# Where the seventh block product of a pair goes in the plain pair behind it

## The chip, the cores and the metric

The kernel runs on one core of a Trainium2 chip. The metric is the time of one execution in device microseconds: the median of three runs was 879.56 us (879.17 to 882.7). One further execution was taken with the hardware profiler.

## The reference, cut to what matters

The kernel computes one layer of a hybrid block on an input of 512 tokens by 1024 channels, in float32. The part that matters here is the feed-forward half at its end:

```
h   = rmsnorm(x, ffn_pre_norm)
up  = causal_dwconv(h @ w_ffn_up, ffn_conv_w, ffn_conv_b)     # (512, 6144), 3 taps
f_gate, f_val = split(up, 2)                                  # 3072 channels each
f   = (gelu(f_gate) * f_val) @ w_ffn_down
x   = x + rmsnorm(f, ffn_post_norm)
```

The rest of the layer (a Mamba-2 mixer, a gated linear recurrence, their gated merge and an output product) runs before it and is not touched.

## The kernel before, in words

**Arithmetic.** Every matrix product is made of three TensorE products. A weight is split into a high part (`whi`, a cast by ScalarE) and the rest (`wlo`, a subtraction by VectorE), the activations likewise, and high by high, high by low and low by high are added in PSUM.

**The up stage.** The up product goes by 24 pairs (`n` = 0 to 23): 128 gate channels and the 128 value channels that belong to them, over 512 tokens. Pairs 0 and 1 go by whole slabs. The others go by blocks: the pair's weights are a 2 by 2 matrix of blocks (a11, a12 for the gate, a21, a22 for the value), the activations are halves of channels and of tokens. There are two ways.

- A *pair of seven* (`seven`, line 1009 on) uses seven block products in place of eight, with sums of blocks as weights (s1, s2, s3, s4) and sums of activations (`comb`). Six stand in its own six slots, in the order a11, s2, s4, s3, a12, s1; each is 12 matmuls of 256 columns. The seventh, a22 times `comb[3]`, is left over: `last_product` adds it into the right half of the pair's bank `z` while the next pair runs.
- A *plain pair* (`eight`, line 1050 on) has four jobs of 12 matmuls of 512 columns: two fill the bank `oa` (gate) and two fill `ob` (value).

Pairs 2 and 3 are plain, and from pair 4 on the pattern is seven, seven, plain: pairs 6, 9, 12, 15, 18 and 21 are plain, and each of them follows a pair of seven. Pair 22 and 23 are pairs of seven.

**What is done for the pair before.** While pair `n` runs, the pair before it (`old`) is finished in four parts: `gate_part` (convolution of the gate: one ScalarE activation, two VectorE taps), `gelu_part`, `last_product` (the TensorE product named above, for a pair of seven alone) and `value_part`. For a pair of seven `value_part` first adds the seventh product to a sum (line 1005, VectorE), then convolves (ScalarE activation, two taps with the weights `negw`), and then multiplies gate and value (line 866). At the end of its own slots a pair of seven makes its two outputs with VectorE: `oa` gets its right half at line 1045, `ob` at line 1046. Line 1046 reads the right half of `z`, into which `last_product` will add.

**Weights.** `w_split` (line 958 on) runs five blocks ahead of the product that uses the block. For a pair of seven VectorE adds s2 = s1 + a11 (line 965) and s4 = s2 + a12 (line 968), ScalarE casts, VectorE subtracts (line 952). The pair's own 1 MB of weights is loaded into one of two halves of a ring named `H` (line 926), issued by SyncE once the half has been read for the last time; s1 and s3 are each loaded as one block and a second block added by a DMA from GpSimd (lines 940 and 942).

**What sets the order.** TensorE and ScalarE run in the order in which the code is written. VectorE's order in this stage is made by a scheduler from the same code, and so can differ from it: it takes line 965 of the second pair ahead early, as the rows show. Each engine works through its own list in order: an instruction that waits holds up all behind it on that engine. In PSUM, line 1031 reads the right half of the bank `x`, whose left half the product with a12 writes next.

Of the kernel before, what the change touches and what calls it, by code (L numbers as in the profile page):

```python
# [56 lines left out]
def block_kernel(ctx: ExitStack, tc, x, slabs, wgate, pc, rows, out):  # L57
# [12 lines left out]
    def ps():  # L70
        return psum.tile([P, S], F32, tag="ps", name="ps")
# [16 lines left out]
    def mm3(acc, lhi, llo, rhi, rlo, start, stop):  # L88
        mm(acc, lhi, rhi, start, False)
        mm(acc, lhi, rlo, False, False)  # L90
        mm(acc, llo, rhi, False, stop)
# [770 lines left out]
    def f_gate(gt):  # L862
        A.activation(gt, gt, AF.Gelu_apprx_tanh)
# [34 lines left out]
    def block_product(out, w, b, start=False):  # L898

        for k in range(HK):  # L900
            c = slice(k * P, (k + 1) * P)
            for e, (u, v) in enumerate(((0, 0), (0, 1), (1, 0))):
                PE.matmul(out, lhsT=w[u][:, c], rhs=b[v][:, k, :], start=start and k == e == 0,
                          stop=k == HK - 1 and e == 2, skip_group_check=not start)
# [86 lines left out]
    def gate_part(n):  # L991
        p = pr[n]
        p["g"] = conv(p["oa"], pcs[:, C_FCW + 3 * n:C_FCW + 3 * n + 3], C_FCB + n, 3)

    def gelu_part(n):
        f_gate(pr[n]["g"])

    def last_product(n):
        if seven_of[n]:
            block_product(pr[n]["z"][:, T1], blk[n]["wa22"], comb[3])  # L1000

    def value_part(n):
        p = pr.pop(n)
        if seven_of[n]:
            V.tensor_add(p["ob"][:, T0], p["u2"], p["z"][:, T1])
            w = negw[:, 3 * n:3 * n + 3]
        else:
            w = pcs[:, C_FCW + 3 * (NF + n):C_FCW + 3 * (NF + n) + 3]
        vt = conv(p["ob"], w, C_FCB + NF + n, 3)
        f_done(n, p["g"], vt)  # L1010
# [38 lines left out]
    def eight(n, old):  # L1049
        p = pr.setdefault(n, {})  # L1050
        for e, o in enumerate(("oa", "ob")):
            p[o] = acc = ps()
            for h in range(2):
                w = blk[n]["wa%d%d" % (e + 1, h + 1)]
                for k in range(HK):
                    c = slice(k * P, (k + 1) * P)
                    mm3(acc, w[0][:, c], w[1][:, c], h2T[0][:, HK * h + k, :],
                        h2T[1][:, HK * h + k, :], h == k == 0, h == 1 and k == HK - 1)
                if old:
                    if e == h == 0:  # L1060
                        gate_part(old)
                    elif e == 0:
                        gelu_part(old)
                        last_product(old)
                    elif h == 0:
                        value_part(old)
                yield

# [42 lines left out]
    for n in range(PLAIN, NF):  # L1111
        for slot, _ in enumerate((seven if seven_of[n] else eight)(n, old)):
            w_split(g + RING - 1)
            g += 1
            if slot == 0:
                pair_load(n + 2)
                pair_sums(n + 2)
            if n == PLAIN and slot in (1, 2):
                h_split(3 * (slot - 1))
            if n < NF - 1:  # L1120
                continue
            if slot == 2:
                stream.update(load=DOWN_SLAB + 2, split=DOWN_SLAB + 2, use=DOWN_SLAB)
                end[0] = slabs.shape[0]
                load_slab()
            elif slot == 3:
                f_split(0)
                f_split(1)
            elif slot == 5:
                f_split(2)  # L1130
                f_split(3)
        old = n
# [100 lines left out]
```

## Time and profile before

| | us |
|---|---|
| median of three runs | 879.56 |
| lowest, highest | 879.17, 882.7 |
| the profiled execution, whole | 882.06 |
| its span from first to last instruction | 880.4 |
| TensorE busy in the span | 864.7 |
| VectorE busy | 587.4 |
| ScalarE busy | 433.6 |

The mean granted TensorE clock was 0.996 of full speed. The profiled execution is 2.5 us above the median; 1.7 us of its time lie around the span. A view of waits names who waited, for whose instruction, and three numbers: microseconds in total, times, longest. A timeline row begins with start and duration in microseconds; in square brackets stands how long the engine was idle before, and what ended that. "PE" is TensorE's matmul, "PEld" its loading of weights, DVE is VectorE, ACT ScalarE. A matmul's row lasts longer than the step to the next row, since matmuls are pipelined: 512 columns follow each other every 0.23 us and 256 columns every 0.12 us.

### The profile page before, as it was taken

To read this page: it belongs to the slowest core of one execution; us is meant where nothing else is said; L and a number is where in the kernel's file an instruction comes from. 1 tells how busy PE (TensorE), PEld (TensorE's weight loads), DVE (VectorE), ACT (ScalarE), POOL (GpSimd) and SP (SyncE) were. 2 spreads that over 40 slices of the span, in tenths; PEclk is the share of its full clock that TensorE was granted. 3 is DMA by queue.
4 is the path that set the end of the run, shared out by engine and by line. 5 is a ranking of instruction groups with operands and counts; after the bars stand their busy time and mean duration, and the time that the engine had idled before them with its cause. 6 is when DMAs were issued, how large, how long until landed. Compare 5 with 4: busy or idle time off the path is not lost.

```text
span 880.4 us, 11591 instructions
## 1 busy us (share of the span) xinstructions
PE 864.7 (98%) x4554; PEld 739.7 (84%) x4554; DVE 587.4 (67%) x909; ACT 433.6 (49%) x714; POOL 28.4 (3%) x44
## 2 busy tenths in 40 slices
PE   7999999999999999999999999999999999999996
PEld 6888887888878888888888989889999899888885
DVE  6777657987875553444466797878978898743225
ACT  6444545578574443322365565445545556633222
POOL 0000000000000000000000101011011000000000
PEclk9999999999999999999999999999999999999999
DMA  6242223222334422222251837466556543422212
GB/s 225 96 146 96 96 94 110 90 84 79 119 103 174 154 96 96 87 99 101 97 191 25 212 127 195 126 180 170 165 144 181 156 127 113 144 96 95 96 48 96
DMA packets 36007, 108.47 MB, mean 123 GB/s; under 512 B 3632, under 2 KB 6896, under 8 KB 35440
## 3 DMA queue, kind: packets, MB, share of 16 engines
q1 hardware_dynamic: 30864, 99.34, 32.7%
q0 software_dynamic: 5088, 8.39, 5.7%
q8 instruction: 35, 0.57, 0.2%
q14 instruction: 20, 0.16, 0.1%
HBM read 103.49 MB, written 2.13 MB: 120 GB/s over the span
## 4 chain that ended last, share of the span: by engine, by line
PE 75%; DVE 11%; DMA 7%; ACT 5%; issue 2%; SPq 0%; DVEq 0%; ACTq 0%
PE ps L53 75%; DMA H<-slabs 5%; DVE wlo L952 2%; DVE tmp L226 2%; ACT whi L53 1%; DVE wlo L183 1%; ACT L L53 1%; DVE L L644 1%; DMA raw<-slabs 1%; ACT tmp L53 1%; DVE tmp L662 1%; DVE raw L965 0%; DMA wg<-wgate 0%; DVE L L638 0%; ACT junk L247 0%
## 5 line engine op out<-in xcount | busy, mean ns | idle before, releaser
L53 PE MATMUL ps<-H,whi 128*128 128x512 f32 x720 | 224.8, 395 | 0.4 <-DVE H L53 0.4
L183 DVE TENSOR_TENSOR wlo<-raw,whi 128x1024 fp32r<-128x1024 f32 x93 | 113.6, 1223 | 117.3 <-ACT whi L53 115.0
L53 ACT CAST whi<-raw 128x1024 fp32r<-128x1024 f32 (+1 forms) x144 | 127.5, 891 | 100.2 <-PE ps L53 96.6
L53 PE MATMUL ps<-C,whi 128*128 128x256 f32 (+1 forms) x656 | 166.5, 335 | 0.1
L53 PEld LDWEIGHTS ps<-H,whi 128*128 128x128 f32 x720 | 134.3, 188 | 30.3 <-issue 2.4
L53 PE MATMUL ps<-H,wlo 128*128 128x512 f32 x352 | 137.5, 391 | 0.4 <-DVE wlo L183 0.4
L53 PEld LDWEIGHTS ps<-C,whi 128*128 128x128 f32 x656 | 112.0, 190 | 12.6 <-DVE quad L1031 0.3
L53 PE MATMUL ps<-C,wlo 128*128 128x512 f32 (+1 forms) x360 | 122.2, 339 | 0.0
L53 PE MATMUL ps<-L,whi 128*128 128x256 f32 (+1 forms) x400 | 87.2, 300 | 0.0
L53 PE MATMUL ps<-whi,H 128*128 128x512 f32 x256 | 81.5, 394 | 0.0
L226 DVE SCALAR_TENSOR_TENSOR tmp<-ps,pcs,tmp 128x511 f32<-128x511 f32 (+2 forms) x100 | 74.5, 745 | 8.1 <-ACT tmp L53 7.2
L53 PEld LDWEIGHTS ps<-H,wlo 128*128 128x128 f32 x352 | 66.2, 188 | 15.3 <-DVE wlo L183 1.2
L53 PEld LDWEIGHTS ps<-C,wlo 128*128 128x128 f32 x360 | 68.3, 190 | 7.6
L53 PEld LDWEIGHTS ps<-L,whi 128*128 128x128 f32 x400 | 64.4, 191 | 2.5
L53 PEld LDWEIGHTS ps<-whi,H 128*128 128x128 f32 x256 | 48.1, 188 | 10.4 <-issue 0.5
L53 ACT ACTIVATE tmp<-tmp 128x512 f32<-128x512 f32 x36 | 22.7, 632 | 55.3 <-DVE tmp L226 55.3
L53 PE MATMUL ps<-wlo,H 128*128 128x512 f32 x128 | 49.8, 389 | 0.0
L952 DVE TENSOR_TENSOR wlo<-H,whi 128x512 fp32r<-128x512 f32 (+1 forms) x46 | 41.1, 894 | 9.7 <-ACT whi L53 9.6
L53 PE MATMUL ps<-L,wlo 128*128 128x256 f32 x168 | 47.5, 283 | 0.0
L53 ACT ACTIVATE tmp<-ps,halfb 128x512 f32<-128x512 f32 x32 | 21.5, 687 | 49.6 <-PE ps L53 49.6
L53 ACT ACTIVATE tmp<-ps,pcs 128x512 f32<-128x512 f32 x40 | 31.0, 776 | 27.9 <-PE ps L53 27.9
L53 PE MATMUL ps<-Y,whi 128*128 128x512 f32 x128 | 40.5, 397 | 0.2 <-DVE Y L200 0.2
(207 smaller groups left out, 1315.3 us busy)
## 6 DMA issues: line engine op xcount, KB each, us to landing
raw<-slabs SPq DMA_DIRECT2D x103, 512.0 KB, 3.2
H<-slabs SPq DMA_DIRECT2D x23, 1024.0 KB, 5.4
raw<-slabs SPq DMA_DIRECT2D x23, 256.0 KB, 3.8
raw<-slabs POOLq DMA_DIRECT2D x23, 256.0 KB, 6.5
quad<-x SPq DMA_DIRECT2D x8, 512.0 KB, 4.2
M<-acsD SPq DMA_DIRECT2D x4, 1024.0 KB, 4.6
out<-tmp SPq DMA_DIRECT2D x8, 256.0 KB, 2.0
third<-slabs SPq DMA_DIRECT2D x5, 256.0 KB, 6.3
```

Source lines behind the costliest of these rows:

```text
L53: return lambda *args, **kw: self.tc.keep_in_program_order(op(*args, **kw))
L183: V.tensor_sub(*late.pop(0))
L226: V.scalar_tensor_tensor(out=t[:, d:], in0=acc[:, :S - d], scalar=w[:, taps - 1 - d:taps - d], in1=t[:, d:], op0=ALU.mult, op1=ALU.add)
L644: V.tensor_tensor_scan(out=qq[:, e, :], data0=aa[:, e, :], data1=uu[:, e, :], initial=0.0, op0=ALU.mult, op1=ALU.add)
L662: V.tensor_mul(gl, gl, hs[i // 4][:, i % 4, :])
L952: V.tensor_sub(lo, src, hi.bitcast(F32))
```

## The change

In `eight`, the parts for the pair before are handed out differently. Before, `gelu_part` and `last_product` both came behind the second job, and `value_part` behind the third. Now the second job is followed by `gelu_part` alone, the third by `last_product`, the fourth by `value_part`. Nothing is added or removed.

```
                     elif e == 0:
                         gelu_part(old)
+                    elif h == 0:
                         last_product(old)
-                    elif h == 0:
+                    else:
                         value_part(old)
```

In plain pair 3, whose `old` is plain, only `value_part` moves. In pairs 6, 9, 12, 15, 18 and 21 `last_product` moves too. Two places in the order show it. Pair numbers do not stand in the rows; the places are those of pair 6.

On TensorE, before, around the leftover product of pair 5 (`ps_4367` is its bank `z`, `a22_4239` its weights); `ps_4485` is `oa` and `ps_4537` is `ob` of pair 6:

```order
L53 MATMUL ps_4485<-C_3363,whi_4066 128x512
L53 MATMUL ps_4485<-C_3364,whi_4066 128x512
L53 MATMUL ps_4485<-C_3363,wlo_4067 128x512
L53 MATMUL ps_4367<-L_4159,a22_4239 128x256 x12
L53 MATMUL ps_4537<-C_3363,whi_4070 128x512
L53 MATMUL ps_4537<-C_3364,whi_4070 128x512
L53 MATMUL ps_4537<-C_3363,wlo_4071 128x512
```

and now, where `ps_4525` is `ob` of pair 6:

```order
L53 MATMUL ps_4525<-C_3363,whi_4070 128x512
L53 MATMUL ps_4525<-C_3364,whi_4070 128x512
L53 MATMUL ps_4525<-C_3363,wlo_4071 128x512
L53 MATMUL ps_4367<-L_4159,a22_4234 128x256 x12
L53 MATMUL ps_4525<-C_3363,whi_4070 128x512
L53 MATMUL ps_4525<-C_3364,whi_4070 128x512
L53 MATMUL ps_4525<-C_3363,wlo_4071 128x512
```

The product has moved behind the third job's 12 matmuls; what stands on either side of it is now the same bank.

On VectorE, the same pair, before; the row ahead of these is line 965 of pair 8, the row behind them line 1031 of pair 7. `tmp_4477` is `ob` of pair 5, `tmp_4551` its value; `tmp_4589` is the gate of pair 6; `wlo_4067` takes s4 and s3 of pair 7, `wlo_4071` its a12 and s1:

```order
L1005 TENSOR_TENSOR tmp_4477<-quad_3967,ps_4367 128x256
L952 TENSOR_TENSOR wlo_4067<-raw_4174,whi_4066 128x512
L968 TENSOR_TENSOR raw_4174<-raw_4174,H_3964 128x512
L226 SCALAR_TENSOR_TENSOR tmp_4551<-tmp_4477,negw_3968,tmp_4551 128x511
L952 TENSOR_TENSOR wlo_4067<-raw_4124,whi_4066 128x512
L226 SCALAR_TENSOR_TENSOR tmp_4551<-tmp_4477,negw_3968,tmp_4551 128x510
L952 TENSOR_TENSOR a22_4239<-H_3964,a22_4239 128x512
L866 TENSOR_TENSOR H_3965<-tmp_4498,tmp_4551 128x512
L952 TENSOR_TENSOR wlo_4071<-H_3964,whi_4070 128x512
L226 SCALAR_TENSOR_TENSOR tmp_4589<-ps_4485,pcs_88,tmp_4589 128x511
L952 TENSOR_TENSOR wlo_4071<-raw_4199,whi_4070 128x512
L226 SCALAR_TENSOR_TENSOR tmp_4589<-ps_4485,pcs_88,tmp_4589 128x510
```

and now, between the same two rows (`tmp_4567` is the value of pair 5):

```order
L952 TENSOR_TENSOR wlo_4067<-raw_4174,whi_4066 128x512
L952 TENSOR_TENSOR wlo_4067<-raw_4124,whi_4066 128x512
L968 TENSOR_TENSOR raw_4174<-raw_4174,H_3964 128x512
L1005 TENSOR_TENSOR tmp_4477<-quad_3967,ps_4367 128x256
L952 TENSOR_TENSOR a22_4234<-H_3964,a22_4234 128x512
L226 SCALAR_TENSOR_TENSOR tmp_4567<-tmp_4477,negw_3968,tmp_4567 128x511
L952 TENSOR_TENSOR wlo_4071<-H_3964,whi_4070 128x512
L226 SCALAR_TENSOR_TENSOR tmp_4567<-tmp_4477,negw_3968,tmp_4567 128x510
L226 SCALAR_TENSOR_TENSOR tmp_4589<-ps_4485,pcs_88,tmp_4589 128x511
L866 TENSOR_TENSOR H_3965<-tmp_4498,tmp_4567 128x512
L226 SCALAR_TENSOR_TENSOR tmp_4589<-ps_4485,pcs_88,tmp_4589 128x510
L952 TENSOR_TENSOR wlo_4071<-raw_4199,whi_4070 128x512
```

The same twelve instructions stand there; line 1005 went from the first to the fourth place, and only one instruction is left between it and the first tap that needs ScalarE's answer to it. On ScalarE the activation of `value_part` went behind the casts of s3 and a22.

## Rows read from the trace of the kernel before

**Rows 1.** The page: busy us, share of the span, instructions.

```profile
PE 864.7 (98%) x4554; PEld 739.7 (84%) x4554; DVE 587.4 (67%) x909; ACT 433.6 (49%) x714; POOL 28.4 (3%) x44
```

**Rows 2.** Busy time by stretch: length, PE, PEld, DVE, ACT, POOL, clock, DMA.

```profile
532.00:747.00 215.00, 212.13 (x1479) 198.06 (x1478) 181.33 (x305) 115.71 (x200) 19.62 (x23) 1.00 0.56 156
```

**Rows 3.** Waits of TensorE, up stage: total us, times, longest.

```profile
PE ps L53 <- DVE tmp L1046: 2.8, 3, 1.1
PEld ps L53 <- DVE tmp L1046: 4.4, 4, 1.5
...
PEld ps L53 <- DVE quad L1031: 0.3, 1, 0.3
```

**Rows 4.** Timeline: leftover products in plain pairs 6, 9, 15, 18, 21.

```profile
557.03 1.70 PE L53 MATMUL ps<-L,a 128*128 128x256 f32 x12 [0.85 <-DVE tmp L1046]
...
589.60 1.69 PE L53 MATMUL ps<-L,a 128*128 128x256 f32 x12 [0.89 <-DVE tmp L1046]
...
652.10 1.70 PE L53 MATMUL ps<-L,a 128*128 128x256 f32 x12
...
684.53 1.70 PE L53 MATMUL ps<-L,a 128*128 128x256 f32 x12 [1.06 <-DVE tmp L1046]
...
715.71 1.60 PE L53 MATMUL ps<-L,a 128*128 128x256 f32 x12
```

**Rows 5.** Timeline of VectorE from plain pair 6 into pair 7.

```profile
553.51 1.22 DVE L952 TENSOR_TENSOR wlo<-H,whi 128x1024 fp32r<-128x1024 f32 x1
...
556.57 0.41 DVE L1046 TENSOR_TENSOR tmp<-ps,quad 128x256 f32<-128x256 f32 x1
...
561.64 0.69 DVE L965 TENSOR_TENSOR raw<-third,H 128x512 f32<-128x512 f32 x1 [2.03 <-DMA H<-slabs]
562.25 0.41 DVE L1005 TENSOR_TENSOR tmp<-quad,ps 128x256 f32<-128x256 f32 x1
562.58 0.68 DVE L952 TENSOR_TENSOR wlo<-raw,whi 128x512 fp32r<-128x512 f32 x1
563.30 0.69 DVE L968 TENSOR_TENSOR raw<-raw,H 128x512 f32<-128x512 f32 x1
563.91 0.74 DVE L226 SCALAR_TENSOR_TENSOR tmp<-tmp,negw 128x511 f32<-128x511 f32 x1
564.57 0.68 DVE L952 TENSOR_TENSOR wlo<-raw,whi 128x512 fp32r<-128x512 f32 x1
...
568.30 0.68 DVE L952 TENSOR_TENSOR wlo<-raw,whi 128x512 fp32r<-128x512 f32 x1
...
569.56 0.41 DVE L1031 TENSOR_TENSOR quad<-quad,ps 128x256 f32<-128x256 f32 x1
...
570.91 1.29 DVE L952 TENSOR_TENSOR wlo<-raw,whi 128x512 fp32r<-128x512 f32 x2 [0.34 <-ACT whi L53]
```

**Rows 6.** Timeline of ScalarE there: value of pair 5.

```profile
562.70 0.82 ACT L53 ACTIVATE tmp<-tmp,pcs,negw 128x512 f32<-128x512 f32 x1 [1.86 <-DVE tmp L1005]
```

**Rows 7.** Timeline of TensorE: pair 7 begins; a12 of pairs 7, 10, 19.

```profile
564.04 0.40 PE L53 MATMUL ps<-C,whi 128*128 128x256 f32 x2
...
570.02 0.51 PE L53 MATMUL ps<-C,whi 128*128 128x256 f32 x2
...
602.43 0.51 PE L53 MATMUL ps<-C,whi 128*128 128x256 f32 x2
...
697.29 0.40 PE L53 MATMUL ps<-C,whi 128*128 128x256 f32 x2
```

**Rows 8.** Timeline of VectorE: line 965 in plain pairs 9 and 18.

```profile
594.04 0.69 DVE L965 TENSOR_TENSOR raw<-raw,H 128x512 f32<-128x512 f32 x1 [1.87 <-DMA H<-slabs]
...
688.63 0.69 DVE L965 TENSOR_TENSOR raw<-raw,H 128x512 f32<-128x512 f32 x1 [1.53 <-DMA H<-slabs]
```

**Rows 9.** DMA issues (count, KB each, us to landing): whole run, then 575:580.

```profile
H<-slabs SPq DMA_DIRECT2D x23, 1024.0 KB, 5.4
...
H<-slabs SPq DMA_DIRECT2D x1, 1024.0 KB, 7.7
```

More of the change, by code (lines that the diff above doesn't have):

```diff
@@ L1063, in eight @@
                         gelu_part(old)
+                    elif h == 0:
                         last_product(old)
-                    elif h == 0:
+                    else:
                         value_part(old)
```

## The prediction

> **What bounds the kernel now.** I read the busy times first: TensorE is busy for 864.7 of 880.4 us [rows 1], and in the up stage with its pairs for 212.13 of 215 us [rows 2], at full clock. So only what makes TensorE stand still there can be won, 2.87 us of this stretch by busy time. Next the waits of TensorE in the up stage [rows 3]: the matmuls wait three times, 2.8 us in all, each time for line 1046, the weight loads four times, 4.4 us. Then the timeline, to see where: the three are the leftover products in the plain pairs 6, 9 and 18 (0.85, 0.89 and 1.06 us), and none stands in a pair of seven [rows 4]. In pairs 12, 15 and 21 the matmul did not wait; 12 is not shown and looks like 21. The reason is that `last_product` adds into the half of `z` that line 1046 reads, and that line runs at 556.57 us in pair 6 [rows 5], when TensorE has already done two jobs.
>
> Why is line 1046 late? VectorE is busy for 181.33 of the 215 us [rows 2], so it is not short of time; it is held up at line 965, which stands early in its list and waits for the load into `H`: 2.03 us in pair 6 [rows 5], 1.87 in pair 9 and 1.53 in pair 18 [rows 8]. Behind such a wait VectorE works without a pause: from 561.64 to the end of line 1031 at 569.97 [rows 5]. And line 1031 is the second place where TensorE meets VectorE: a12 of pair 7 begins at 570.02, 0.05 us behind its end [rows 5, 7], and its weight load waited 0.3 us for it [rows 3]. Pair 7 begins at 564.04 [rows 7]; four products of 12 matmuls at 0.12 us make 5.76, so TensorE would have reached a12 at 569.80.
>
> **The change part by part.** Counts of instructions and bytes stay as they are; only order changes.
>
> *The leftover product one job later on TensorE.* A job is 12 matmuls at 0.227, 2.72 us. Line 1046 ends 0.85 to 1.06 us after TensorE wants it, so with 2.72 us of other work in front the wait goes in all three places, and the short one of the weight load in pair 15. That takes away 2.8 us by the matmul rows, 4.4 by the weight loads, and the third job must be able to start earlier: its last weights, the 1024-wide subtraction in pair 6, are done at 554.73 [rows 5], and TensorE will want them at about 556.0. That cover is 1.3 us; were it gone, the wait would only change its name. So pair 7 begins about 1.0 us earlier, at 563.0, and reaches a12 at 568.8.
>
> *VectorE's list up to line 1031.* This is what is late next. Line 965 cannot move: its load was issued before anything changed in this pair. From 561.64 I set the new order in steps between rows [rows 5]: 0.61 for an addition of 512 columns, 0.60 for a subtraction, 0.66 for a tap, 0.33 for one of 256 columns. Line 965 at 561.64; two subtractions at 562.25 and 562.85; line 968 at 563.45; line 1005 at 564.06; the subtraction of a22 at 564.39. The first tap of the value needs ScalarE: its activation began 0.45 us after line 1005 began and took 0.82 [rows 5, 6], so the tap can start 1.30 after line 1005, at 565.36, and VectorE stands still for 0.37 us. Before, a subtraction and line 968 lay in between and covered it. Then the tap, a subtraction (566.02), two taps (566.62, 567.28), line 866 (567.94), a tap (568.54), the subtraction of s1 (569.20), and line 1031 at 569.80. From line 965 that is 8.16 us, where it was 7.92: 0.37 more for the wait, and 0.12 less, since line 968 no longer follows directly the subtraction that reads its buffer (0.72 before, 0.60 else). Line 1031 then ends at 570.21 and a12 begins at 570.26, against 570.02. So in pair 6 the microsecond taken away is lost again 14 us later, with 0.24 on top: TensorE waits 1.4 us in pair 7 instead of 1 us in pair 6.
>
> At this place a rule decides whether that wait is real, as the two touch different halves of the bank. The row shows a start 0.05 us behind the end of line 1031, and in pair 10 a12 at 602.43 is likewise 0.05 behind it, if line 1031 stands 7.93 behind line 965 there as in pair 6 [rows 7, 8]. The Trainium skill, PSUM — Partial Sum Buffer, section "PSUM bank collisions raise a hardware error", says to guard PSUM by bank and quadrant and not by address; the trace agrees. By an address rule the sum would be the whole 2.8 to 4.4 us.
>
> *Behind line 1031.* The pair of subtractions at 570.91 waited 0.34 us for ScalarE, whose gelu waits for the last gate tap [rows 5]. That tap comes at 568.54 now, was at 568.90 (569.56 less a tap), so the pair can start at 569.80 + 0.33 + 0.60 = 570.73 without a pause: VectorE leaves the plain pair 0.18 us earlier. Its later subtraction of a12 releases the half of `H` for the load that holds line 965 next time, so the chain of VectorE and loads comes round 0.18 earlier per plain pair, if the loads take as long as now.
>
> *The end.* Where TensorE last waits sets the gain; in pair 21 no leftover product waits [rows 4]. In pair 18 line 965 stood at 688.63 [rows 8]; four plain pairs ahead of it give 0.72, so 687.91; with 8.16 + 0.41 + 0.05 a12 of pair 19 begins at 696.53, against 697.29 [rows 7]. TensorE is there in time, since the 1.06 it waited in pair 18 alone brings it to 696.2. That is 0.76 us less. Without the 0.72 it would be 697.25, no gain. In pair 21 I see no wait: its leftover product came in time [rows 4]. In pair 3 only the value moves, and TensorE does not wait there: nothing.
>
> Instructions moved on the way cost nothing by the same list: s1's subtraction is later by 0.90 (568.30 to 569.20), done at 569.88, and TensorE wants s1 at 570.26 + 1.44 at the earliest; a12's subtraction is earlier by about a microsecond, so one load into `H` starts earlier.
>
> The sum is −0.8 us: the profiled execution's 882.06 would be 881.3, and the median 879.56 becomes 878.8. The profiled one is 2.5 above the median, a shift that I leave in both.
>
> **The rivals.**
>
> *The wait goes and nothing replaces it.* Line 1031 would have to come a microsecond earlier, through loads that land earlier (5.4 us is their median, 7.7 the one issued at 576 [rows 9]), or a12 would have to start without it. For it: three matmul waits clearly named [rows 3]. Against it: two a12 starts right behind line 1031. It gives −2.8 to −4.4, about 876.0.
>
> *The loads collide and the chain gets longer.* The later end of s1's subtraction releases a buffer of s1 0.90 us later; its next copy and the addition by GpSimd behind it move towards the next load into `H`. That they share is visible: the load at 576 took 7.7 us where the median is 5.4 [rows 9]. The Trainium skill, DMA: Bandwidth & Descriptors, section "Issuing engines are not separate DMA queues", says that transfers of all issuing engines run on the same 16 DMA engines and interleave; that row fits. If the load lands later by the 0.90, the chain is longer by 0.90 − 0.18 = 0.72 per plain pair instead of shorter, and after four of them a12 of pair 19 starts at 688.63 + 2.88 + 8.62 = 700.13, 2.8 us later than now: 882.4. It decides as soon as a load loses more than 0.18 us. Against it: the load ahead of that copy starts a microsecond earlier, so the copy need not land later.
>
> *The change does not take the wait away*, because line 1046 gets later by more than 1.7 us. VectorE's list ahead of it is unchanged in pair 6, so this needs a longer chain first: 879.6.
>
> **How the numbers follow.** Forecast 0.64 (−0.8; its own range −1.8 to +0.6), nothing in place 0.14, colliding loads 0.17, no effect 0.05. About 0.5%, 4.4 us, is what a measurement of this kernel can tell from no change, and none of the cases except the upper end of the first rival reaches it. Faster by more than that means under 875.2: 0.05. Slower means over 884.0, the second rival at more than one and a half times its price, or two mishaps: 0.05. The same: 0.90. The range is from the middle of the first rival's span to near the second's price: 876.3 to 882.0.
>
> **What would show it.** Right, if the profile after names no wait for line 1046 in a plain pair, and in its place waits for line 1031 at a12 of pairs 7 and 10, 1.0 to 1.6 us each; if line 1031 begins 8.1 to 8.2 us behind line 965 in pairs 6, 9 and 18; if VectorE has a pause of some 0.4 us in front of the first `negw` tap, for ScalarE; and if the pause in front of the two subtractions behind line 1031 is gone. Wrong, if TensorE's busy share of the stage rises by over 2 us with no new wait, or if the time between loads into `H` gets longer from one plain pair to the next.

## The result, and the profile after

The changed kernel takes 889.88 us, the median of six runs (888.19 to 891.85); the kernel before takes 879.75 in six runs beside them (877.94 to 882.7). The ratio is 1.0112, 95% interval [1.0095, 1.0128]: slower by about 10 us, where 0.8 us less was forecast. The profiled execution of the kernel after is its fastest, 888.19 us; that of before, 882.06, is near the upper end of its runs. So the two traces show 6.1 us of the difference, and the rest of the ten is in neither.

First the page and the busy times of the up stage, the views of [rows 1] and [rows 2] (us, share or count; in the second row the length, the engines, the granted clock, the DMA share):

```profile
PE 866.8 (98%) x4554; PEld 742.1 (84%) x4554; DVE 586.2 (66%) x909; ACT 434.7 (49%) x714; POOL 28.4 (3%) x44
...
532.00:747.00 215.00, 208.49 (x1444) 195.88 (x1444) 175.38 (x297) 110.60 (x191) 19.58 (x23) 0.98 0.55 156
```

Within the same 215 us TensorE is busy 3.6 us less than in [rows 2] and issues 35 matmuls fewer. It stands still more, and elsewhere than before; these are its waits in the stage, to be laid beside [rows 3]:

```profile
PE ps L53 <- DVE quad L1031: 6.4, 4, 2.8
...
PEld ps L53 <- DVE quad L1031: 7.5, 5, 3.0
```

The wait for line 1046 is gone. Line 1031 has taken its place: 6.4 us in four waits against 2.8 in three. They stand at the a12 products of pairs 7, 10, 13 and 16 (start, duration, and in brackets the wait), as [rows 7] of before:

```profile
570.25 0.66 PE L53 MATMUL ps<-C,whi 128*128 128x256 f32 x2 [2.76 <-DVE quad L1031]
...
603.79 0.39 PE L53 MATMUL ps<-C,whi 128*128 128x256 f32 x1 [0.71 <-DVE quad L1031]
...
636.00 0.39 PE L53 MATMUL ps<-C,whi 128*128 128x256 f32 x1 [0.87 <-DVE quad L1031]
...
669.37 0.78 PE L53 MATMUL ps<-C,whi 128*128 128x256 f32 x2 [2.03 <-DVE quad L1031]
```

Why is line 1031 late? VectorE from plain pair 6 into pair 7, the stretch of [rows 5]:

```profile
561.61 0.69 DVE L965 TENSOR_TENSOR raw<-third,H 128x512 f32<-128x512 f32 x1 [2.11 <-DMA H<-slabs]
562.22 1.29 DVE L952 TENSOR_TENSOR wlo<-raw,whi 128x512 fp32r<-128x512 f32 x2
563.42 0.69 DVE L968 TENSOR_TENSOR raw<-raw,H 128x512 f32<-128x512 f32 x1
564.02 0.41 DVE L1005 TENSOR_TENSOR tmp<-quad,ps 128x256 f32<-128x256 f32 x1
564.36 0.69 DVE L952 TENSOR_TENSOR a<-H,a 128x512 fp32r<-128x512 f32 x1
565.33 0.75 DVE L226 SCALAR_TENSOR_TENSOR tmp<-tmp,negw 128x511 f32<-128x511 f32 x1 [0.28 <-ACT tmp L53]
...
569.18 0.68 DVE L952 TENSOR_TENSOR wlo<-raw,whi 128x512 fp32r<-128x512 f32 x1
569.77 0.42 DVE L1031 TENSOR_TENSOR quad<-quad,ps 128x256 f32<-128x256 f32 x1
...
570.71 1.29 DVE L952 TENSOR_TENSOR wlo<-raw,whi 128x512 fp32r<-128x512 f32 x2
```

From line 965 to line 1031 it is 8.16 us. That was in the forecast. What was not is where line 965 itself comes to stand. In pair 6 it is at 561.61 (561.64 in [rows 5]). From there on it falls back; in pairs 9 and 18 (to be laid beside [rows 8]), and the last two of the stage, for pairs 22 and 23:

```profile
595.16 0.69 DVE L965 TENSOR_TENSOR raw<-raw,H 128x512 f32<-128x512 f32 x1 [2.13 <-DMA H<-slabs]
...
692.28 0.69 DVE L965 TENSOR_TENSOR raw<-raw,H 128x512 f32<-128x512 f32 x1 [1.22 <-DMA H<-slabs]
...
716.01 0.69 DVE L965 TENSOR_TENSOR raw<-third,H 128x512 f32<-128x512 f32 x1 [2.74 <-DMA H<-slabs]
...
724.08 0.69 DVE L965 TENSOR_TENSOR raw<-raw,H 128x512 f32<-128x512 f32 x1
```

The last two of them in the kernel before:

```profile
709.72 0.69 DVE L965 TENSOR_TENSOR raw<-third,H 128x512 f32<-128x512 f32 x1
717.73 0.68 DVE L965 TENSOR_TENSOR raw<-raw,H 128x512 f32<-128x512 f32 x1
```

So line 965 is 1.12 us late in pair 9, 3.65 in pair 18 and 6.35 at the end: about the 6.1 us that the spans differ by (886.5 and 880.4). TensorE meets the late chain once more, in pair 22, where line 1031 and a12 stand 0.05 us apart and the weight load waits 0.34 us:

```profile
732.94 0.42 DVE L1031 TENSOR_TENSOR quad<-quad,ps 128x256 f32<-128x256 f32 x1
...
733.41 0.50 PE L53 MATMUL ps<-C,whi 128*128 128x256 f32 x2
```

What VectorE waited for in the stage, first before and then after:

```profile
DVE raw L965 <- DMA H<-slabs: 14.8, 9, 2.7
...
DVE tmp L226 <- ACT tmp L53: 4.3, 7, 0.6
```

```profile
DVE raw L965 <- DMA H<-slabs: 23.1, 11, 4.0
...
DVE tmp L226 <- ACT tmp L53: 6.0, 13, 0.6
```

The wait for ScalarE that I had added by hand is there, and small. The loads into `H` cost 8.3 us more. Over the whole run the median of such a load rose from 5.4 us [rows 9] to

```profile
H<-slabs SPq DMA_DIRECT2D x23, 1024.0 KB, 6.8
```

and the 17 loads issued between 550 and 735 us, added one by one, took 111.3 us from issue to landing where they took 101.8.

The loads themselves are the same. What differs is what was already on the way when they were issued. The extreme case is the load for pair 22 (703 to 708 us): GpSimd's additions, SyncE's issue, and its landing time, first before:

```profile
704.75 1.72 POOL L942 DMA_DIRECT2D raw<-slabs  x2 [8.55 <-DMA raw<-slabs]
...
703.28 0.38 SPq L926 DMA_DIRECT2D H<-slabs  x1
...
H<-slabs SPq DMA_DIRECT2D x1, 1024.0 KB, 5.1
```

and after:

```profile
705.44 0.84 POOL L942 DMA_DIRECT2D raw<-slabs  x1 [7.32 <-DMA raw<-slabs]
707.10 0.85 POOL L942 DMA_DIRECT2D raw<-slabs  x1 [0.82 <-DMA raw<-slabs]
...
706.75 0.38 SPq L926 DMA_DIRECT2D H<-slabs  x1
...
H<-slabs SPq DMA_DIRECT2D x1, 1024.0 KB, 9.2
```

Before, both additions were issued behind the load, the first by 1.47 us (an earlier one had 0.58 us left when the load went out); now one is 1.31 us ahead of it and one 0.35 behind. Of the 17 loads 9 were issued while an addition was under way before, and 13 after. With none under way a load took 5.1 us in the mean before and 5.0 after; with one or more, 6.7 and 7.0. But the count does not give the price: in three of the four loads that changed sides the addition is only 0.03 to 0.11 us ahead, and they take 0.2 to 0.3 us longer than before. Load by load, 8.1 of the 9.5 us lie in four, issued at 576.08, 609.62, 620.32 and 706.75 us (1.1, 1.5, 1.5 and 4.1 us longer). In these an addition went out 1.1 to 1.5 us ahead of the load, where before the same one had gone out behind it or at most 0.5 us ahead. Over both traces, a load took 6.0 to 9.2 us with an addition 0.37 to 2.13 us ahead, and 4.6 to 5.9 otherwise. Not all of it reaches TensorE: line 965 waits 2.74 us for the load at 706.75, and the weight load in pair 22 only the 0.34 us named above.

### The profile page after: what moved, and what is told of

Same layout as the page of the kernel before. It is cut to its first block, busy times and chain, and to the rows that moved or that the text cites. A ratio compares the mean times of both kernels' runs of the same rounds, so it can differ in the third digit from the quotient of the medians.

```text
span 886.5 us, 11591 instructions
## 1 busy us (share of the span) xinstructions
PE 866.8 (98%) x4554; PEld 742.1 (84%) x4554; DVE 586.2 (66%) x909; ACT 434.7 (49%) x714; POOL 28.4 (3%) x44
## 3 DMA queue, kind: packets, MB, share of 16 engines
HBM read 103.49 MB, written 2.13 MB: 119 GB/s over the span
## 4 chain that ended last, share of the span: by engine, by line
PE 65%; DVE 17%; DMA 9%; ACT 6%; issue 2%; SPq 0%; DVEq 0%; ACTq 0%
PE ps L53 65%; DMA H<-slabs 8%; DVE wlo L952 4%; DVE tmp L226 4%; ACT tmp L53 2%; ACT whi L53 1%; ACT L L53 1%; DVE wlo L183 1%; DVE L L644 1%; DMA raw<-slabs 1%; DVE raw L968 1%; ACT L53 1%; DVE Y L866 1%; DVE tmp L662 0%; DVE L L638 0%
## 5 line engine op out<-in xcount | busy, mean ns | idle before, releaser
L53 PE MATMUL ps<-C,whi 128*128 128x256 f32 (+1 forms) x656 | 168.8, 339 | 6.5 <-DVE quad L1031 6.4
```

Of the source, the lines that this page charges most:

```text
L53: return lambda *args, **kw: self.tc.keep_in_program_order(op(*args, **kw))
```

## The experiments

Three theories stood against each other. L: the loads into `H` land later, because additions (and the copies ahead of them) now go out in front of them. S: the value's convolution stands later in the order, and by that alone line 1031 comes late. P: the new place of the leftover product on TensorE is what costs, through the stalls at line 1031 and the lower clock behind them. Each run has its own runs of the kernel before on the same chip, 879.8 to 880.2 us; ratios are to these.

**One half at a time.** Only the product moves, in front of `value_part` but behind the third job:

```
                         gelu_part(old)
-                        last_product(old)
                     elif h == 0:
+                        last_product(old)
                         value_part(old)
```

> Half of the change: the leftover product behind the third job, the value part still behind the third job too, right after it. ScalarE's list is that of the kernel before; VectorE's is made anew by the scheduler and differs at a few places. Theory L (the loads into H land later because the new order of casts and subtractions sends the copies and adds of s1 and s3 ahead of them): ScalarE's list is the old one, so the loads issued beside the adds land as before (mean about 7 us, against 8.3 in the changed kernel) and the time is 877 to 883. Rival P (the product's place on TensorE alone does it, by waits of over 2 us at line 1031 and the half clock behind them): 887 to 892, with these waits.

Measured: 884.06 us, 1.0041 [1.0017, 1.0065]. Only the value moves:

```
                         last_product(old)
-                    elif h == 0:
+                    elif h == 1:
                         value_part(old)
```

> The other half: the leftover product stays behind the second job, the value part goes behind the fourth. ScalarE's list is that of the changed kernel. Theory L: the loads into H land late as in the changed kernel (7.4 to 9.2 us beside the adds) and the time is 886 to 892. Rival P: 878 to 882, with the waits for line 1046 back at 2 to 3 us and nothing else lost.

Measured: 886.4 us, 1.0078 [1.0053, 1.0103]; its profiled execution took 880.35 us, 6 us under that, and so shows little of the loss. Neither half carries it alone. In the first one VectorE's list got longer between line 965 and line 1031; in pairs 6 and 7

```profile
562.52 0.69 DVE L965 TENSOR_TENSOR raw<-third,H 128x512 f32<-128x512 f32 x1 [2.06 <-DMA H<-slabs]
...
572.01 0.41 DVE L1031 TENSOR_TENSOR quad<-quad,ps 128x256 f32<-128x256 f32 x1
```

that is 9.49 us, where it was 7.92, and TensorE waits there for up to 3.9 us. Its time lies between the two ranges expected, and that of the second half in theory L's. Each half gives VectorE another list, so the pair of runs says that both edits cost, not by which mechanism.

**No additions at all.** Both kernels without GpSimd's additions, which leaves the second summand out of s1 and s3:

```
-        for q, one, two in adds:
-            G.dma_start(out=b[q], in_=drawn(n, *two), accum_op=ALU.add)
```

> The kernel before without the adds that GpSimd issues for s1 and s3: these two hold only their first block, so the values are wrong and 28 transfers of 256 KB are gone. Theory L: loads into H land in 5 to 6 us everywhere, line 965 waits little, time 874 to 879. Rival P and a rival S (the value part's exposed wait on VectorE is what costs): 876 to 880, the difference to the next kernel is what counts.

> The changed kernel without the adds that GpSimd issues for s1 and s3 (values wrong likewise). Theory L: within 2.5 us of the kernel before without adds, since nothing is left that stands ahead of the loads into H. Rivals P and S: 7 to 11 us above it, as with the adds.

Measured: 877.22 us for the kernel before, 0.9969 [0.9955, 0.9984], and 877.37 for the kernel after, 0.9963 [0.9948, 0.9978]. VectorE's list hardly changes (7 and 9 of its 909 rows stand elsewhere than in the kernel each comes from), and TensorE's not at all. The ten microseconds between the two orders are gone. In the changed kernel without additions the loads between 550 and 735 us, and the only wait for one at the line that was 965:

```profile
H<-slabs SPq DMA_DIRECT2D x17, 1024.0 KB, 4.8
```

```profile
DVE raw L963 <- DMA H<-slabs: 0.2, 1, 0.2
```

No matmul and no weight load waits for VectorE there. Without the additions the new order costs nothing; so neither theory S nor theory P, by itself, holds for this kernel.

**The additions, but behind the load.** The additions stay, all of them. For the second pair of seven GpSimd first copies one column of the load that must go ahead, and so waits for its landing (line numbers rise by four):

```
+        if i % 2:
+            seen = tiny.tile([P, 1], F32, tag="seen", name="seen", bufs=2)
+            GO.tensor_copy(seen, blk[n - 1]["raw"][:, 2 * D - 1:2 * D])
         for q, one, two in adds:
-            G.dma_start(out=b[q], in_=drawn(n, *two), accum_op=ALU.add)
+            GO.dma_start(out=b[q], in_=drawn(n, *two), accum_op=ALU.add)
```

> The changed kernel, with GpSimd's list in written order and, ahead of the adds of the second pair of seven of each group of three (pairs 5, 8, 11, ...), a copy of one element of the load into H of the pair ahead of it, so that these adds go out only when that load has landed. Nothing else changes and the values are right. Theory L (an add ahead of a load into H makes it land later, and VectorE waits for it at line 965): the loads into H of pairs 10, 13, 16, 19 and 22 land in 5.0 to 6.5 us against 7.4 to 9.2, and the time is 877 to 884. Rival P (the product's place on TensorE: waits at line 1031, half clock): 887 to 892. If the adds merely collide with the next load instead: 884 to 890, with late loads for pairs 11, 14, ...

Measured: 879.05 us, 0.9978 [0.9953, 1.0002]. The lists of VectorE, ScalarE and TensorE are the changed kernel's row for row; only the times at which GpSimd's additions go out differ (those held back, and those behind them on GpSimd's list), and the whole loss is gone. TensorE's matmuls wait for nothing in the stage. The waits of GpSimd's new copy and of VectorE:

```profile
POOL seen L53 <- DMA H<-slabs: 79.9, 6, 14.6
...
DVE raw L969 <- DMA H<-slabs: 12.3, 6, 3.1
```

12.3 us in place of 23.1. The loads' median is 5.4 us again. What I expected of single loads was too low: five still take 6.6 to 7.9 us, issued with additions under way, mostly the three that had been held back; the others land in 4.7 to 6.1. This is the run on which the explanation rests.

The same gate on the kernel before:

> The kernel before, with GpSimd's additions for the second pair of seven held behind the load into H of the pair before it, as in the run that took the changed kernel back to 879.05. Theory L (the loss comes from additions that go out ahead of a load): in the kernel before only part of the loads are overtaken, so it gains little: 876 to 879, line 965 waits 8 to 13 us for the loads (14.8 in the kernel before). Rival: the gate itself is worth several us whatever the order of the parts; then 870 to 874. Or the gate costs something by itself (additions late, TensorE waits for s1): 881 to 884.

Measured: 878.15 us, 0.9998 [0.9981, 1.0016]; line 965 waits 11.0 us for loads there and TensorE's matmuls for nothing. So the gate gives the kernel before nothing that can be measured, and is no gain of its own that hid the loss. With it the two orders are within a microsecond (878.15 and 879.05).

**The bank that line 1031 guards.** The halves of `x` in banks of their own, in the changed kernel:

```
-        x, z = ps(), ps()
+        x, x1, z = ps(), ps(), ps()
...
-block_product(x[:, T1], b["ws2"], comb[1])
+block_product(x1[:, T1], b["ws2"], comb[1], True)
...
-V.tensor_add(p["u2"], p["u2"], x[:, T1])
+V.tensor_add(p["u2"], p["u2"], x1[:, T1])
```

> The changed kernel with the two halves of x in PSUM banks of their own, so that the product with a12 no longer waits for line 1031, which reads the other half. Theory L: VectorE and the loads are the longer chain, so TensorE stands elsewhere (casts and subtractions of s1, line 1046); loads into H land as late as before, time 884 to 889. Rival P: the waits of 6.4 us at line 1031 and the half clock behind them are gone, and with them the loss: 878 to 882.

Measured: 889.05 us, 1.011 [1.0087, 1.0133]: no change. The waits at line 1031 are gone, and with them two stretches at the lower clock (below), and TensorE waits for other work of VectorE instead:

```profile
PE ps L53 <- DVE wlo L952: 5.2, 10, 1.0
```

A loss of this size can therefore come without a stall at line 1031 and without the lower clock (granted clock 0.999 over the run). But the run does not show that it is the same loss, since VectorE's list changed with the edit (some 70 of its 909 rows stand elsewhere): line 1031 now stands 9.2 to 9.4 us behind line 965 in five of the six plain pairs. The loads add up to 100.6 us, and line 965 waits 14.2 us for them, no more than in the kernel before (101.8 and 14.8), so theory L's late loads are not here either. What rules theory P out are the runs above, without the additions and with them held back: TensorE's order there is the changed kernel's, and the loss is gone.

**VectorE in the written order.** The scheduler off in the loop over pairs (`V.on = True` in front of it), first the kernel after, then before:

> The changed kernel with VectorE's list of the stage in written order: line 965 of the next pair of seven no longer stands ahead of the value of the pair before, so nothing waits behind its load. Theory L: a load that lands late holds up nothing, 876 to 881. Rival S (the value part behind the fourth job with its exposed wait on ScalarE, and line 1031 later, is what costs): 885 to 892.

> The kernel before with VectorE's list of the stage in written order. Theory L: 876 to 880, within 2 us of the changed kernel in written order. Rival S: 878 to 881, with the changed one 5 us or more above it.

Measured: 882.82 us, 1.0045 [1.0029, 1.0061], and 877.16, 0.9976 [0.9961, 0.999]. In neither does VectorE wait for a load any more; it still does not make them equal, and neither theory's numbers held for the first. TensorE's waits in the first one (line 1031 stands under a helper's line here); in the second there is none:

```profile
PE ps L53 <- DVE quad L53: 3.4, 6, 0.6
```

Six waits, one in each of six pairs: theory S, at 4.4 us by the steps between the matmuls (0.73 each). To see whether that needs the additions, the changed kernel in written order without them:

> The changed kernel with VectorE in the written order, and without GpSimd's additions to s1 and s3, which leaves out the second summand of those two sums. Theory S (in the written order line 1031 comes late by the order alone, 0.73 us in six places): 879.5 to 882.5, with waits of TensorE at line 1031 of some 0.7 us in six pairs. Theory L (also here the loads beside the additions make it late): 876 to 878.5 and no such waits.

Measured: 884.57 us, 1.0051 [1.0031, 1.0071], and the same six waits:

```profile
PE ps L53 <- DVE quad L53: 3.5, 6, 0.6
```

Here S is right, though the time is 2.1 us above the range that I gave it, and L is wrong. So there are two costs, not one: with VectorE in the written order the later value part delays line 1031 by itself; the scheduler's order, which the real kernels have, avoids that (no wait without the additions) and pays through the loads instead.

Last, the kernel before in the written order with the additions behind the load:

> The kernel before with VectorE in the written order and the additions held behind the load. In the written order nothing of VectorE waited for the loads any more, so theory L says that holding back the additions adds nothing: 876.5 to 878, as without it (877.16). Rival: the loads still set a wait of another engine there; then below 876.

Measured: 877.39 us, 0.9971 [0.9951, 0.9991]. As expected the gate adds nothing where VectorE waits for no load, although the median load is 6.2 us there: a late load costs only what waits for it. Of the kernels that compute everything the kernel before in written order has the lowest median, 877.16 us, 0.24% faster than before [0.1%, 0.39%]; this last one is level with it.

## Why the prediction was wrong

*The wait for line 1046 goes.* Right: no row of it is left, and pairs 6, 9 and 18 lose it.

*Line 965 to line 1031 takes 8.16 us, and a12 of pair 7 begins at 570.26.* Right: 8.16, in five of the six plain pairs, and 570.25. The pause for ScalarE was 0.28 us instead of 0.37. TensorE waited 2.76 us there and not 1.4, since in this run it came 1.3 us earlier already from work ahead of pair 6. In pair 10 the wait was 0.71, under the 1.0 to 1.6 that I gave.

*The pause behind line 1031 goes, and VectorE leaves the plain pair 0.18 us earlier.* The pause is gone: the two subtractions began at 570.71 (forecast 570.73), 0.20 us earlier than in [rows 5].

*"So the chain of VectorE and loads comes round 0.18 earlier per plain pair, if the loads take as long as now."* This step failed: it carried the landing time of the loads into `H` over unchanged. They took 9.5 us more over 17 loads, and line 965 came later by 6.35 us at the end of the stage instead of earlier by 0.72 in pair 18. The condition was written down and not worked out, although rows 9 already held a load of 7.7 us beside one of 5.4. The prediction's own sign of being wrong came with it: the loads issued in the plain pairs stood 31.6 us apart in the mean before, and 32.9 after.

*"Instructions moved on the way cost nothing".* Only the subtractions of s1 and a12 were followed. In the prediction's own list that of s3 moved as well, from 564.57 to 562.85, and it frees a buffer: SyncE sends the next copy right behind its end, first before and then after:

```profile
565.28 0.33 SPq L940 DMA_DIRECT2D raw<-slabs  x1
```

```profile
563.53 0.33 SPq L940 DMA_DIRECT2D raw<-slabs  x1
```

*The rival with the colliding loads* named the right mechanism at 882.4 and 0.17, with the wrong cause. I let the additions come later, behind a later subtraction of s1, and argued against it that the load ahead starts earlier. In the first round the trace shows the reverse: what VectorE does earlier frees buffers earlier, and additions end up further in front of the load that line 965 waits for. The copy at 563.53 instead of 565.28 brought its addition to 568.04 instead of 568.90. The copy behind them did go out later, as the rival has it (569.89 instead of 569.01), but landed at 573.97 instead of 575.19, and so its addition was issued at 574.56 instead of 575.78, while the load that follows it moved only from 576.28 to 576.08 and took 8.8 us instead of 7.7. Once the chain is late, it is the load that falls back: at 620.32 and 706.75 it went out 1.96 and 3.47 us later than before, the addition ahead of it only 0.79 and 0.69 later. The price too was wrong: not 0.90 in every round, but 1.1 to 4.1 us in four loads and next to nothing in most others.

The Trainium skill, DMA: Bandwidth & Descriptors, section "Issuing engines are not separate DMA queues", says that transfers interleave on the same 16 DMA engines whichever engine started them. The trace agrees, and gives the price: 4.8 us for 1 MB with no addition in the stage, 6.7 and 7.0 in the mean, before and after, with additions of 256 KB under way when it is issued.

*The chances.* 0.05 for slower by over 0.5% rested on the second rival at its own price. But what it moves is an order of issues, and here a shift of 1.2 us in it (0.10 behind the load to 1.07 ahead) made a load 1.5 us longer; there was no reason to cap it near the 0.90.

Open: the 4 us by which the medians differ more than the two profiled runs do; where the loss with banks of their own comes from; the shares of the two halves, which cost 3.9 and 6.2 us when made alone; and the 5.7 us between the two kernels in written order, of which 4.4 are seen.

## What to carry to other kernels

When an edit lets an engine finish something earlier, list what that releases, down to the transfers, and look whether any of them now goes out ahead of the one that the bound waits for: being early can cost more than being late. In this kernel the order of DMAs issued by different engines followed from buffer releases, and an edit elsewhere flipped it; letting the others wait for the one load on the critical chain took the whole loss back, and changed nothing measurable in the kernel that had no such loss. And a forecast that holds "if the loads take as long as now" needs the price of the case where they don't, at the size that the slowest load in the trace shows.

## What was not expected of the hardware

Behind two of the waits at line 1031 TensorE ran on at its lower clock. The changed kernel, granted clock in the last column but two:

```profile
570.00:574.00 4.00, 3.75 (x18) 3.75 (x19) 4.00 (x8) 3.62 (x7) 0.00 (x0) 0.57 0.80 228
669.00:673.00 4.00, 3.63 (x17) 3.63 (x18) 4.00 (x8) 3.52 (x8) 0.00 (x0) 0.57 0.85 256
```

and the matmuls behind the first of them:

```profile
570.70 0.41 PE L53 MATMUL ps<-C,wlo 128*128 128x256 f32 x1
570.91 0.63 PE L53 MATMUL ps<-C,whi 128*128 128x256 f32 x2
571.34 0.41 PE L53 MATMUL ps<-C,wlo 128*128 128x256 f32 x1
```

Three matmuls take 0.64 us here, 0.213 each, against 0.12 at full speed: 1.2 GHz instead of 2.4. This lasted about 17 matmuls, 1.6 us lost each time, behind waits of 2.76 and 2.03 us; behind those of 0.71 and 0.87 the clock stayed. By rows, 3.6 us more of waiting and twice 1.6 of slow matmuls make 6.8, a little over the 6.1 by which the spans differ. The slow matmuls are how part of the delay appears rather than where it comes from: in pair 22 TensorE had just met the late line 1031 again, so without them it would have waited there. The other surprise was how steady the 1 MB load is with no addition in the stage: 4.65 to 4.95 us in the changed kernel (in the kernel before two of 17 took 5.7 and 6.1), where beside them it takes 4.7 to 9.2.
